# A hybrid decoder trunk on one core: the output projection's residual added by accumulating DMAs, with the banks copied out by ScalarE

## The chip, the cores and the metric

The kernel runs on one core of a Trainium2 chip. The metric is the time of one execution on the device in microseconds. The engines are TensorE (PE, with its weight loads as PEld), VectorE (DVE), ScalarE (ACT), GpSimd (POOL) and SyncE (SP). DMAs are issued here from SP's queue and from POOL's queue, and all run on the core's 16 DMA engines.

## The reference

Two layers of a trunk with 512 tokens and 2048 channels, all in float32. Each layer normalises x, projects it once, runs three groups of heads beside each other, and projects their gated outputs back onto x:

```python
for l in range(DEPTH):
    h = rmsnorm(x, norm_w[l])
    proj = jnp.einsum("bsd,de->bse", h, w_in[l])
    (ssd_z, ssd_xbc, ssd_dt, cfm_a, cfm_g, cfm_z,
     att_q, att_k, att_v, att_z) = jnp.split(proj, split_idx, axis=-1)
    y_ssd = ssd_branch(ssd_z, ssd_xbc, ssd_dt, ...)
    y_cfm = conformer_branch(cfm_a, cfm_g, cfm_z, ...)
    y_att = diff_attention_branch(att_q, att_k, att_v, att_z, ...)
    y = jnp.concatenate([y_ssd, y_cfm, y_att], axis=-1)
    x = x + jnp.einsum("bse,ed->bsd", y, w_out[l])
```

The change touches the last line: the sum of x and the output projection.

## The kernel before

Channels lie on the partitions. x is held as 16 blocks of 128 channels by 512 tokens, each in two parts whose sum is exact, `xh[k]` and `xl[k]` (`put_x`: ACT casts the block to `xh`, DVE subtracts to get `xl`, and the squares are summed for the norm).

All projections go through `project`. It fills four PSUM banks of 128 x 512 (`ps_p`, four buffers in all) from 16 blocks of the contraction, in eight steps of two blocks. For each step 512 KB of weights are loaded from SP's queue into `wraw` (two buffers), ACT scales and casts them to `wh` and DVE computes the remainder `wl` (four buffers each, so two steps), and PE runs 24 matmuls (lines 186 to 188): two blocks, four banks, three products of parts. In the last step the matmuls are sorted by bank, so that bank 0 is complete first and bank 3 last. The next chunk starts with a step in which each of the first 12 matmuls in turn reopens banks 0 to 3, three each, so a bank has to be emptied before its turn.

Work beside the projections is handed to `project` as a list of jobs, which are issued between the steps. The order of PE is that in which the code issues; on the other engines a scheduler of the framework orders instructions by priority and by its own estimate of when their inputs are there. `urgent()` raises the priority of weight splits and of the emptying of banks.

The output projection of a layer is four chunks (`dc`) of four blocks. Before the change, the job `res` has DVE add `xh[k]` and `xl[k]` into a tile `t` of the pool `rw` (four buffers) while the chunk is computed (line 774). When bank `b` is complete, DVE adds it to that tile (line 783). In layer 1 the tile is stored to `out` from SP (line 785). In layer 0 it is the new block of x: in the next chunk `dt_mm` multiplies the chunk's four tiles with the 16 columns for dt of the next layer (line 263, eight rows on PE in the trace, after the first step), and then four jobs `put_x` split them. The last chunk's tiles go into the first projection of layer 1 in the same way.

The instructions that the change concerns, in the file's words:

```python
for b in range(4):
    k = 4 * dc + b
    with urgent():
        V.tensor_tensor(ts[b], ts[b], banks[b], ALU.add)
    if l == DEPTH - 1:
        nc.sync.dma_start(out=out[k], in_=ts[b])
    else:
        jobs.append(lambda k=k, t=ts[b]: put_x(k, t))
```

Of the kernel before, what the change touches and what calls it, by code (L numbers as in the profile page):

```python
# [8 lines left out]
F32 = mybir.dt.float32  # L9
F32R = mybir.dt.float32r  # L10
AF = mybir.ActivationFunctionType
ALU = mybir.AluOpType
AX = mybir.AxisListType

P = 128
S = 512
D = 2048
KB = D // P
DEPTH = 2
EPS = 1e-6  # L20
NEG = -1e30
LEAD = 2000
# steps between the stages of what runs beside the projections
PL0, PL1, CL, QL, AL0, AL1, H0, HP, HL = 1, 2, 2, 2, 3, 1, 1, 5, 2
WARM = 2
TCUT, NPAD = (0, 7, 12, 18, 22, 26, 29, 32), 2

# one column chunk of the input projection per row: name, first column
CH_BC, CH_X0, CH_X1, CH_A, CH_G, CH_CZ, CH_Q, CH_K, CH_V, CH_AZ, CH_Z0, CH_Z1 = range(12)
CHUNK_COL = (2048, 1024, 1536, 2576, 3088, 3600, 4112, 4624, 5136, 5648, 0, 512)  # L30

# columns of the packed per-partition parameters
PP_CW, PP_CB, PP_SN, PP_FW, PP_FB, PP_LW, PP_LB, PP_SL = 0, 48, 60, 68, 192, 196, 200, 204
PP_N = 205
# columns of the packed row parameters (one layer)
RP_DTB, RP_AL, RP_QW, RP_KW, RP_LAM = 0, 16, 32, 96, 160
RP_N = 416
# columns of the constants
C_ID, C_TRI, C_STR, C_AM, C_ONE, C_DTS, C_ROPE = 0, 128, 256, 384, 512, 640, 656
C_N = 656 + 4 * 64  # L40

# [2 lines left out]
def kernel(  # L44
# [57 lines left out]
    sqx = [None]  # L102

    def add_sq(k, src):
        """The squares of x, summed over the blocks."""
        if k == 0:
            sqx[0] = lt([P, S], "rb")
            A.activation(sqx[0], src, AF.Square)
        else:
            t = sa()  # L110
            A.activation(t, src, AF.Square)
            V.tensor_tensor(sqx[0], sqx[0], t, ALU.add)

    def put_x(k, src):
        """x in two exact parts."""
        split(xh[k], xl[k], src)
        add_sq(k, src)

    pace, pace_hi = [None], [None]

    def weights(src, scales, raw=None, between=None):
        """Two 128-row blocks of weights: scaled by the row, in two exact parts."""
        with urgent():
            if raw is None:
                raw = wraw.tile([P, 2, S], F32, tag="wraw", name="wraw")
                nc.sync.dma_start(out=raw, in_=src)
            res = []
            for j in range(2):
                if j and between:
                    between()  # L130
                h = wsp.tile([P, S], F32R, tag="wh", name="wh")
                lo = wsp.tile([P, S], F32R, tag="wl", name="wl")
                if scales[j] is None:
                    split(h, lo, raw[:, j, :])
                else:
                    pace_hi[0] = A.activation(h, raw[:, j, :], AF.Copy, scale=scales[j]).ins  # L136
                    pace[0] = V.scalar_tensor_tensor(lo, raw[:, j, :], scales[j], h.bitcast(F32), ALU.mult,  # L137
                                                     ALU.subtract).ins
                res.append((h, lo))
        return res  # L140
# [1 line left out]
    clock, queue = [0], []  # L142

    def after(n, fn):
        """Issue fn n steps of the projections later."""
        queue.append((clock[0] + n, fn))

    def paced(fn):
        """Not before this step's weights are split."""
        with tc.issue_after(pace[0]):  # L150
            fn()

# [13 lines left out]
                fn()  # L166

    def project(src, order, act, scales, cm, jobs=(), pre=None):
        """Four [128, 512] sums over the 16 blocks; cm: channels on the partitions, else tokens.
        Jobs, and what they left for later, are issued between the steps."""  # L170
        banks = [ps_p.tile([P, S], F32, tag="ps_p", name="ps_p") for _ in range(4)]
        N = KB // 2
        for n, kk in enumerate(order):
            wt = weights(src[kk], scales[2 * kk:2 * kk + 2], *(pre(kk) if pre else ()))
            tick()
            order_jb = [(j, b) for j in range(2) for b in range(4)]
            if n == N - 1:
                order_jb.sort(key=lambda jb: jb[1])
            for j, b in order_jb:
                k = 2 * kk + j  # L180
                first, last = n == 0 and j == 0, n == N - 1 and j == 1
                h, lo = wt[j]
                ah, al = act[k]
                c = blk(b)
                if cm:
                    T.matmul(banks[b], h[:, c], ah, start=first, stop=False)  # L186
                    T.matmul(banks[b], h[:, c], al, start=False, stop=False)  # L187
                    T.matmul(banks[b], lo[:, c], ah, start=False, stop=last)  # L188
                else:
                    T.matmul(banks[b], ah[:, c], h, start=first, stop=False)  # L190
                    T.matmul(banks[b], ah[:, c], lo, start=False, stop=False)  # L191
                    T.matmul(banks[b], al[:, c], h, start=False, stop=last)  # L192
            for job in jobs[len(jobs) * n // N:len(jobs) * (n + 1) // N]:
                job()
        return banks

    def rsqrt_bcast(acc, n, tag):
        """1/sqrt(mean + eps) of column sums of squares, on every partition."""
        ps = psm()
        T.matmul(ps, ones, acc, start=True, stop=True)  # L200
        r = lt([P, S], tag)
        A.activation(r, ps, AF.Sqrt, scale=1.0 / n, bias=epst)
        V.reciprocal(r, r)
        return r

    # ---- parameters
    nc.sync.dma_start(out=nwt, in_=nw)
    # the array's clock rises while it waits for the first blocks
    z = sa()
    with tc.high_priority(2 * LEAD):  # L210
        V.memset(z, 0.0)
# [12 lines left out]
    first, xraw = [], []  # L224

    def load_x(kk, w):
        """Two blocks of x; the first two take turns with their weights."""
        if kk == 4:
            load_params()
        for k, t in first:  # L230
# [15 lines left out]
        split(xh[0], xl[0], first[0][1])  # L246
        return raw, lambda t=first[1][1]: split(xh[1], xl[1], t)

    # ---- the 16 dt columns, four blocks of x at a time side by side in the columns of the array
    psd, wd = [None], [None]  # L250

    def dt_load(l):
# [14 lines left out]
    for l in range(DEPTH):  # L267
# [47 lines left out]
        lead[0] = True  # L315

        def evac(banks, pad=0, rstd=rstd):
            """The banks times 1/rms(x), for channels on the partitions."""
            res = []
            with urgent():  # L320
                for b in banks:
# [4 lines left out]
                    res.append(t)  # L326
            return res

        # ---- dt = softplus(raw + bias), log1p by the series of atanh; a = -exp(a_log) dt and its sums
        sm64 = lambda tag: lt([P, 4, 16], tag)  # L330
        dt, s1, s2, s3, a_t, acs, dec, cdec = (sm64(n) for n in ("dt", "s1", "s2", "s3", "a_t", "acs", "dec", "cdec"))
        acr = [None]
# [42 lines left out]
            acr[0] = dram.tile([16, S], F32, name="acr")  # L375
            G.dma_start(out=acr[0], in_=r)

        # ---- causal convolution of x, B, C: channels on the partitions
        def conv4(raw, ci, dst, col=col):
            w = lambda j: col(PP_CW + 4 * ci + j)  # L380
            V.tensor_scalar(dst, raw[:, 3:3 + S], w(3), None, ALU.mult)
# [46 lines left out]
            after(CL, state)  # L428

        def ssd_pair(i, l=l, xs=xs, st=st, xdt=xdt, cbm=cbm, cT=cT, acs=acs, acr=acr):  # L430
            """Heads 2 i and 2 i + 1: within the chunks, then from the states before them."""
            g, j = i // 4, i % 4
            ms = [big.tile([P, S], F32, tag=f"o{2 * (i % 2) + half}", name="m") for half in range(2)]
            e = wt2()
# [47 lines left out]
        raws = evac(banks, 3)  # L482
        g1 = [lambda i=i, raws=raws: conv_x(i, raws) for i in range(4, 8)] + ssd_jobs(1)

        # ---- conformer: a * sigmoid(g), convolution, layer norm, silu
        u, ca = [], []
        banks = in_proj(CH_A, True, g0[8:] + g1[0:4])
        with urgent():
# [51 lines left out]
                V.tensor_tensor(ca[i], ca[i], rl, ALU.mult)  # L540
                A.activation(ca[i], ca[i], AF.Silu, scale=col(PP_LW + i), bias=col(PP_LB + i))

        # ---- attention: q, k normed and rotated, then transposed
        tabs = [None, None]

        def qk_tab(n, row=row, tabs=tabs):
# [54 lines left out]
        xq = evac_t(banks)  # L601
        banks = in_proj(CH_K, False, mix([ahead(lambda t=t, xq=xq: qk_norm(0, t, xq[t])) for t in range(4)], tp[1]))
        xk = evac_t(banks)
        # ---- differential attention over the keys up to each block of queries
        v, o = [], [None] * 4
        parts = [None] * 4

        def head(h, qk=qk, parts=parts):
            """q and k of one head in two exact parts: for each half, q high and low on the two halves of the
            partitions, k high on both, k low on both."""  # L610
            for half in range(2):
                own, other = slice(half * 64, half * 64 + 64), slice(64 - half * 64, 128 - half * 64)
                q_, k_ = qk[0][own, h, :], qk[1][own, h, :]
# [72 lines left out]
                A.activation(vt, banks[t], AF.Copy, scale=rstd_t[:, t:t + 1])  # L686
                v.append(vt)

        # ---- gate of the SSD group
        sqy = [None]  # L690

        def silus(raws):
# [68 lines left out]

        cjobs = [lambda raws=raws: silus(raws)] + [lambda i=i: cfm_out(i) for i in range(4)]

        # ---- output projection and residual
        sls = lt([P, 1], "sls")
        V.tensor_scalar(sls, col(PP_SL), 1.0 - lam_init, None, ALU.mult)
        out_scales = [col(PP_SN + i) for i in range(8)] + [None] * 4 + [sls] * 4
        jobs = cjobs + ([lambda l=l: dt_load(l + 1)] if l < DEPTH - 1 else [])
        for dc in range(4):
            ts = []  # L770

            def res(k, ts=ts):
                t = rw()
                V.tensor_tensor(t, xh[k].bitcast(F32), xl[k].bitcast(F32), ALU.add)
                ts.append(t)

            jobs = jobs + [lambda k=4 * dc + b, res=res: res(k) for b in range(4)]
            banks = project([w_out[l, dc, kk] for kk in range(KB // 2)], (0, 1, 2, 3, 6, 7, 4, 5), yact, out_scales, True, jobs)
            jobs = [lambda dc=dc, ts=ts: dt_mm(dc, ts)] if l < DEPTH - 1 else []
            for b in range(4):  # L780
                k = 4 * dc + b
                with urgent():
                    V.tensor_tensor(ts[b], ts[b], banks[b], ALU.add)
                if l == DEPTH - 1:
                    nc.sync.dma_start(out=out[k], in_=ts[b])
                else:
                    jobs.append(lambda k=k, t=ts[b]: put_x(k, t))
        late = jobs


# [59 lines left out]
```

## Time and profile before

| what | value |
|---|---|
| time, median of 3 runs | 1552.81 us (1552.58 to 1553.71) |
| span of the profiled execution | 1550.5 us |
| median of the runs less that span (what lies around the span) | 2.3 us |
| PE busy | 1543.9 us (100%) |
| PE weight loads busy | 1265.2 us (82%) |
| DVE busy | 1093.0 us (70%) |
| ACT busy | 719.1 us (46%) |
| POOL busy | 42.7 us (3%) |
| DMA from SP's queue | 143.75 MB, 30.9% of 16 engines |
| DMA from POOL's queue | 11.87 MB, 2.8% of 16 engines |

The profile is that of one execution; the span runs from its first to its last instruction. No total of that execution is listed beside its span, so the median of the runs stands for it. Busy shares are means over the whole span. A PE that is busy all the time is not at its peak: matmuls are pipelined, so a row lasts 0.39 us while the next one starts 0.23 us after it. Where PE has no idle time, its starts tell when a tile is needed.

### The profile page before, as it was taken

The page shows a single profiled execution, that of the slowest core. Times are in us where ns is not written, and L with a number is a line of the kernel's source. Part 1 is how long each engine was busy: PE and PEld are TensorE (multiplying, and loading weights), DVE is VectorE, ACT ScalarE, POOL GpSimd, SP SyncE. Part 2 cuts the span into 40 slices and gives each one's busy share as a digit, 9 for nine tenths or more (in the row PEclk, how much of TensorE's full clock was granted, in tenths as well). Part 3 has the DMA queues.
Part 4 walks back from the last instruction along what each step waited for, and adds up shares of the span by engine and source line. Part 5 has one row for each costly group of instructions (what it writes and reads, how often), then busy time and mean ns, then how long its engine had stood idle before and what let it go on. Part 6 is the DMA issues. An engine that isn't in the chain of part 4 may idle for free.

```text
span 1550.5 us, 19452 instructions
## 1 busy us (share of the span) xinstructions
PE 1543.9 (100%) x7220; PEld 1265.2 (82%) x7220; DVE 1093.0 (70%) x2040; ACT 719.1 (46%) x1176; POOL 42.7 (3%) x80
## 2 busy tenths in 40 slices
PE   9999999999999999999999999999999999999998
PEld 6788888888888888888888888888888888888887
DVE  7665756989698889543447667579897988883332
ACT  7442525334576667333244335253435766662221
POOL 0010100000000000000000101010000000000000
PEclk9999999999999999999999999999999999999999
DMA  7243333333322232333333434332333222334442
GB/s 244 82 134 94 112 115 113 94 96 87 100 76 79 82 86 96 95 96 95 95 95 85 131 87 133 101 113 88 96 96 87 77 82 83 83 94 123 124 126 76
DMA packets 47262, 156.85 MB, mean 101 GB/s; under 512 B 6496, under 2 KB 7392, under 8 KB 47168
## 3 DMA queue, kind: packets, MB, share of 16 engines
q1 hardware_dynamic: 42656, 143.75, 30.9%
q0 software_dynamic: 4512, 11.87, 2.8%
q8 instruction: 56, 0.92, 0.3%
q14 instruction: 38, 0.31, 0.1%
HBM read 151.34 MB, written 4.26 MB: 100 GB/s over the span
## 4 chain that ended last, share of the span: by engine, by line
PE 99%; DVE 0%; DMA 0%; issue 0%; SPq 0%; ACT 0%; DVEq 0%
PE ps_p L186 23%; PE ps_p L188 22%; PE ps_p L187 22%; PE ps_p L192 8%; PE ps_p L190 8%; PE ps_p L191 8%; PE ps_s L456 2%; PE ps_s L664 1%; PE ps_s L461 1%; PE ps_s L421 1%; PE ps_s L635 1%; PE ps_s L634 1%; PE ps_s L656 1%; PE ps_s L591 0%; PE ps_s L410 0%; PE ps_s L263 0%
## 5 line engine op out<-in xcount | busy, mean ns | idle before, releaser
L136 ACT ACTIVATE wh<-wraw,nwt 128x512 fp32r<-128x512 f32 x384 | 275.6, 722 | 459.6 <-PE ps_p L187 265.4
L186 PE MATMUL ps_p<-xh,wh 128*128 128x512 f32 x1024 | 411.8, 402 | 0.8 <-DVE rw L325 0.4
L188 PE MATMUL ps_p<-xh,wl 128*128 128x512 f32 x1024 | 400.4, 391 | 0.4 <-DVE wl L137 0.4
L187 PE MATMUL ps_p<-xl,wh 128*128 128x512 f32 x1024 | 399.6, 390 | 0.0
L137 DVE SCALAR_TENSOR_TENSOR wl<-wraw,nwt,wh 128x512 fp32r<-128x512 f32 x384 | 285.6, 748 | 152.1 <-ACT wh L136 149.3
L186 PEld LDWEIGHTS ps_p<-xh,wh 128*128 128x128 f32 x1024 | 192.8, 188 | 48.7 <-ACT wh L136 7.9
L187 PEld LDWEIGHTS ps_p<-xl,wh 128*128 128x128 f32 x1024 | 192.9, 188 | 41.4 <-issue 3.8
L188 PEld LDWEIGHTS ps_p<-xh,wl 128*128 128x128 f32 x1024 | 192.4, 188 | 41.8 <-DVE wl L137 1.1
L190 PE MATMUL ps_p<-wh,xh 128*128 128x512 f32 x512 | 202.8, 396 | 0.0
L192 PE MATMUL ps_p<-wh,xl 128*128 128x512 f32 x512 | 199.9, 390 | 0.0
L191 PE MATMUL ps_p<-wl,xh 128*128 128x512 f32 x512 | 199.6, 390 | 0.0
L510 DVE SCALAR_TENSOR_TENSOR ca<-u,ppt,ca 128x512 f32<-128x512 f32 x240 | 179.3, 747 | 2.9
L192 PEld LDWEIGHTS ps_p<-wh,xl 128*128 128x128 f32 x512 | 96.1, 188 | 20.3
L190 PEld LDWEIGHTS ps_p<-wh,xh 128*128 128x128 f32 x512 | 96.3, 188 | 18.9
L191 PEld LDWEIGHTS ps_p<-wl,xh 128*128 128x128 f32 x512 | 96.3, 188 | 18.8
L186 PE MATMUL ps_p<-ysh,wh 128*128 128x512 f32 x256 | 100.9, 394 | 0.0
L187 PE MATMUL ps_p<-ysl,wh 128*128 128x512 f32 x256 | 99.9, 390 | 0.0
L188 PE MATMUL ps_p<-ysh,wl 128*128 128x512 f32 x256 | 99.8, 390 | 0.0
L136 ACT ACTIVATE wh<-wraw,ppt 128x512 fp32r<-128x512 f32 x64 | 46.0, 722 | 85.5 <-PE ps_p L187 79.0
L137 DVE SCALAR_TENSOR_TENSOR wl<-wraw,ppt,wh 128x512 fp32r<-128x512 f32 x64 | 47.4, 747 | 49.6 <-ACT wh L136 49.5
L100 DVE TENSOR_TENSOR wl<-wraw,wh 128x512 fp32r<-128x512 f32 x32 | 22.2, 693 | 63.4 <-ACT wh L99 63.4
L137 DVE SCALAR_TENSOR_TENSOR wl<-wraw,sls,wh 128x512 fp32r<-128x512 f32 x32 | 24.0, 751 | 51.8 <-ACT wh L136 51.8
(450 smaller groups left out, 2013.5 us busy)
## 6 DMA issues: line engine op xcount, KB each, us to landing
wraw<-w_in SPq DMA_DIRECT2D x191, 512.0 KB, 3.6
wraw<-w_out SPq DMA_DIRECT2D x64, 512.0 KB, 3.6
m<-acr POOLq DMA_DIRECT2D x32, 256.0 KB, 4.3
xraw<-xT SPq DMA_DIRECT2D x16, 256.0 KB, 5.2
out<-rw SPq DMA_DIRECT2D x16, 256.0 KB, 2.7
wT<-acr POOLq DMA_DIRECT2D x32, 96.0 KB, 3.8
wraw<-w_in SPq DMA_DIRECT2D x2, 256.0 KB, 3.9
cst<-consts SPq DMA_DIRECT2D x1, 456.0 KB, 6.9
```

The source lines that it names most:

```text
L100: V.tensor_tensor(lo, src, hi.bitcast(F32), ALU.subtract)
L136: pace_hi[0] = A.activation(h, raw[:, j, :], AF.Copy, scale=scales[j]).ins
L137: pace[0] = V.scalar_tensor_tensor(lo, raw[:, j, :], scales[j], h.bitcast(F32), ALU.mult, ALU.subtract).ins
L186: T.matmul(banks[b], h[:, c], ah, start=first, stop=False)
L187: T.matmul(banks[b], h[:, c], al, start=False, stop=False)
L188: T.matmul(banks[b], lo[:, c], ah, start=False, stop=last)
L190: T.matmul(banks[b], ah[:, c], h, start=first, stop=False)
L191: T.matmul(banks[b], ah[:, c], lo, start=False, stop=False)
L192: T.matmul(banks[b], al[:, c], h, start=False, stop=last)
L421: T.matmul(ps, st[g][:, 3, blk(c)], dsx, start=True, stop=True)
L456: T.matmul(yd[half * 64:half * 64 + 64, blk(c)], xdt[g][c][:, hh:hh + 64], ms[half][:, blk(c)], start=True, stop=True)
L510: V.scalar_tensor_tensor(ca[i], u[i][:, j:j + S], w(j), ca[i], ALU.mult, ALU.add)
```

## The change

In all chunks but the last of layer 1, ACT copies the bank into the tile. In layer 0 a DMA from POOL's queue then adds the block of the input x to the tile, reading `xT` from memory (`accum_op=ADD` into the tile); the tile is used as before, and SP also stores it to `out`. In layer 1 the DMA from POOL's queue adds the tile onto what layer 0 has stored in `out`. The last four blocks of layer 1 keep the two adds on DVE, with the sum of the parts of x in tiles of the pool `big` (`xs_last`).

```diff
-        for dc in range(4):
-            ts = []
...
-            def res(k, ts=ts):
-                t = rw()
-                V.tensor_tensor(t, xh[k].bitcast(F32), xl[k].bitcast(F32), ALU.add)
-                ts.append(t)
...
-            jobs = jobs + [lambda k=4 * dc + b, res=res: res(k) for b in range(4)]
+        xs_last = []
+
+        def res(k, xs_last=xs_last):
+            t = big.tile([P, S], F32, tag=f"o{k % 4}", name="xlast")
+            V.tensor_tensor(t, xh[k].bitcast(F32), xl[k].bitcast(F32), ALU.add)
+            xs_last.append(t)
+
+        for dc in range(4):
+            jobs = jobs + [(lambda b=b: res(12 + b)) if l == DEPTH - 1 and dc == 3 else (lambda: None) for b in range(4)]
+            ts = []
...
+            last = l == DEPTH - 1 and dc == 3
             for b in range(4):
                 k = 4 * dc + b
+                t = rw()
                 with urgent():
-                    V.tensor_tensor(ts[b], ts[b], banks[b], ALU.add)
-                if l == DEPTH - 1:
-                    nc.sync.dma_start(out=out[k], in_=ts[b])
-                else:
-                    jobs.append(lambda k=k, t=ts[b]: put_x(k, t))
+                    if last:
+                        V.tensor_tensor(t, xs_last[b], banks[b], ALU.add)
+                        nc.sync.dma_start(out=out[k], in_=t)
+                    else:
+                        A.copy(t, banks[b])
+                        if l < DEPTH - 1:
+                            G.dma_start(out=t, in_=xT[k], accum_op=ALU.add)
+                            nc.sync.dma_start(out=out[k], in_=t)
+                        else:
+                            G.dma_start(out=out[k], in_=t, accum_op=ALU.add)
+                ts.append(t)
+                if l < DEPTH - 1:
+                    jobs.append(lambda k=k, t=t: put_x(k, t))
```

How it changes the order on ACT, at the end of the first chunk of layer 0's output projection. Before (the first two rows are the weight split of the next chunk's first step; `xh_91` to `xh_94` are blocks 0 to 3 of x; in brackets are the semaphores that a row waits for, by engine or DMA queue):

```order
L136 ACTIVATE wh<-wraw,ppt 128x512 [waits DMAHW2_49,DVE_49,PE_49]
L136 ACTIVATE wh<-wraw,ppt 128x512 [waits DVE_49,PE_49]
L99 CAST xh_91<-rw 128x512 [waits DVE_49]
L108 ACTIVATE rb<-rw 128x512
L99 CAST xh_92<-rw 128x512 [waits DVE_49]
L111 ACTIVATE sa<-rw 128x512
L136 ACTIVATE wh<-wraw,ppt 128x512 [waits DMAHW3_49,PE_49,Activation_49]
```

The same place after; a DMASW semaphore is that of a DMA from POOL's queue:

```order
L136 ACTIVATE wh<-wraw,ppt 128x512 [waits DMAHW2_49,DVE_49,PE_49]
L136 ACTIVATE wh<-wraw,ppt 128x512 [waits DVE_49,PE_49]
L790 COPY rw<-ps_p 128x512 [waits PE_49] x3
L136 ACTIVATE wh<-wraw,ppt 128x512 [waits DMAHW3_49,DVE_49,PE_49]
L99 CAST xh_91<-rw 128x512 [waits DMASW7_49]
L790 COPY rw<-ps_p 128x512 [waits PE_49]
L136 ACTIVATE wh<-wraw,ppt 128x512 [waits DVE_49]
L108 ACTIVATE rb<-rw 128x512
L99 CAST xh_92<-rw 128x512 [waits DMASW0_49]
```

Three banks are copied, then half of a weight split, then the cast of block 0 with a wait for its accumulating DMA, and only then the copy of the fourth bank and the other half of the split.

On PE, the dt matmuls after the first step of the next chunk, before (the rows follow the step's last matmul):

```order
L188 MATMUL ps_p<-ysh_5127,wl 128x512
L263 MATMUL ps_s<-rw,wd 32x512 [waits PE_49]
L263 MATMUL ps_s<-rw,wd 32x512 x3
L186 MATMUL ps_p<-ysh_5170,wh 128x512 [waits Activation_49]
L187 MATMUL ps_p<-ysl_5171,wh 128x512
```

and after:

```order
L188 MATMUL ps_p<-ysh_5127,wl 128x512
L263 MATMUL ps_s<-rw,wd 32x512 [waits DMASW7_49,PE_49]
L263 MATMUL ps_s<-rw,wd 32x512 [waits DMASW0_49]
L263 MATMUL ps_s<-rw,wd 32x512 [waits DMASW1_49]
L263 MATMUL ps_s<-rw,wd 32x512 [waits DMASW2_49]
L186 MATMUL ps_p<-ysh_5170,wh 128x512
```

Nothing moved on PE; each dt matmul now waits for the DMA of its own block.

On SP's queue, where before there were weight loads alone in layer 0's output projection, the stores of the four blocks now stand among them (the loads are those of steps 1 to 5 of the second chunk):

```order
L126 DMA wraw_5676<-w_out 128x1024 [waits DMAHW0_49,DVE_49]
L126 DMA wraw_5715<-w_out 128x1024 [waits DMAHW1_49,DVE_49]
L126 DMA wraw_5753<-w_out 128x1024 [waits DMAHW2_49,DVE_49]
L793 DMA out<-rw_5656 128x512 [waits DMASW7_49]
L793 DMA out<-rw_5660 128x512 [waits DMASW0_49]
L793 DMA out<-rw_5664 128x512 [waits DMASW1_49]
L126 DMA wraw_5792<-w_out 128x1024 [waits DMAHW3_49,DVE_49]
L793 DMA out<-rw_5668 128x512 [waits DMASW2_49]
L126 DMA wraw_5831<-w_out 128x1024 [waits DMAHW4_49,DVE_49]
```

The load of the fourth step follows three stores, that of the fifth a fourth store.

## Rows read from the trace of the kernel before

**Rows 1.** The page, busy time, share of the span, and instructions of an engine.

```profile
span 1550.5 us, 19452 instructions
PE 1543.9 (100%) x7220; PEld 1265.2 (82%) x7220; DVE 1093.0 (70%) x2040; ACT 719.1 (46%) x1176; POOL 42.7 (3%) x80
```

**Rows 2.** Waits of PE: line, who was waited for: total us, times, longest.

```profile
PE ps_s L215 <- DVE sa L211: 1.5, 1, 1.5
...
PE ps_p L186 <- ACT wh L136: 0.4, 1, 0.4
```

**Rows 3.** Busy time by stretch, layer 0's output projection, its four chunk seams.

```profile
core 0: us, PE busy (x) PEld busy (x) DVE busy (x) ACT busy (x) POOL busy (x), PEclk, DMA share, GB/s
646.00:691.00 45.00, 45.00 (x202) 36.25 (x201) 21.08 (x32) 15.59 (x25) 0.00 (x0) 1.00 0.32 94
...
781.00:826.00 45.00, 45.00 (x200) 35.95 (x199) 23.59 (x40) 16.38 (x24) 2.14 (x4) 1.00 0.31 94
```

**Rows 4.** The chain that ended last: start us, us, what; the dt matmuls.

```profile
652.01 0.99 PE ps_s L263 x8
...
786.67 1.00 PE ps_s L263 x8
```

**Rows 5.** Timeline of PE at the first seam: start us, us, engine, line, operation.

```profile
642.00 0.39 PE L188 MATMUL ps_p<-ych,wl 128*128 128x512 f32 x1
...
646.14 0.39 PE L188 MATMUL ps_p<-ych,wl 128*128 128x512 f32 x1
646.37 0.40 PE L186 MATMUL ps_p<-ysh,wh 128*128 128x512 f32 x1
...
648.45 0.39 PE L186 MATMUL ps_p<-ysh,wh 128*128 128x512 f32 x1
...
651.94 1.07 PE L263 MATMUL ps_s<-rw,wd 128*32 128x512 f32 x8
652.94 0.50 PE L186 MATMUL ps_p<-ysh,wh 128*128 128x512 f32 x1
```

**Rows 6.** Groups by line, DVE: busy us, mean ns | idle before, releaser.

```profile
L783 DVE TENSOR_TENSOR rw<-rw,ps_p 128x512 f32<-128x512 f32 x32 | 22.0, 686 | 15.5 <-PE ps_p L188 14.7
...
L774 DVE TENSOR_TENSOR rw<-xh,xl 128x512 f32<-128x512 f32 x32 | 20.5, 687 | 0.6 <-DMA out<-rw 0.6
```

**Rows 7.** Line 423, ACT's copy of a bank: duration ns min/median/max, first and last start.

```profile
L423 ACT COPY st<-ps_s x4: 586/588/589, 144.8 to 995.0; 128x512 f32<-128x512 f32 x4
```

**Rows 8.** Timeline at the end of the kernel.

```profile
1542.40 0.69 DVE L783 TENSOR_TENSOR rw<-rw,ps_p 128x512 f32<-128x512 f32 x1 [5.73 <-PE ps_p L188]
...
1543.12 4.47 SPq L785 DMA_DIRECT2D out<-rw  x4
```

**Rows 9.** Timeline of DVE at the first seam: banks 0 and 2.

```profile
642.43 0.69 DVE L783 TENSOR_TENSOR rw<-rw,ps_p 128x512 f32<-128x512 f32 x1
...
645.19 0.69 DVE L783 TENSOR_TENSOR rw<-rw,ps_p 128x512 f32<-128x512 f32 x1
```

**Rows 10.** Timeline of ACT at the first seam.

```profile
643.15 0.62 ACT L99 CAST xh<-rw 128x512 fp32r<-128x512 f32 x1 [1.60 <-DVE rw L783]
643.68 0.63 ACT L108 ACTIVATE rb<-rw 128x512 f32<-128x512 f32 x1
```

**Rows 11.** Line 437, loads of 256 KB from POOL's queue; the page's table of issues.

```profile
m<-acr POOLq DMA_DIRECT2D x32, 256.0 KB, 4.3
...
DMA to landing us min/median/max: 3.3/4.3/6.9
```

**Rows 12.** DMA issues of 85 to 87 us and of 89 to 90 us.

```profile
m<-acr POOLq DMA_DIRECT2D x1, 256.0 KB, 3.8
...
m<-acr POOLq DMA_DIRECT2D x1, 256.0 KB, 6.4
```

**Rows 13.** DMA rate in 40 slices of 640 to 665 us.

```profile
GB/s 0 0 0 0 0 105 203 393 138 0 0 0 0 0 0 164 249 361 66 0 0 0 0 177 256 321 85 0 0 0 0 0 0 111 164 374 184 7 0 0
```

**Rows 14.** The page's table of issues: weight loads, KB each, us to landing.

```profile
wraw<-w_out SPq DMA_DIRECT2D x64, 512.0 KB, 3.6
```

## What the change will do: the prediction

> **What bounds the kernel now.** I read the page first: TensorE (PE) is busy for 1543.9 of 1550.5 us [rows 1]. Then who kept PE waiting: four waits, between 1.5 us and 0.4 us, all in the start-up [rows 2]. Then the stretches that the change touches: in each of the four 45 us slices of layer 0's output projection (the first and the last stand) PE is busy for 45.00 us, while VectorE (DVE) is busy for about 21 and ScalarE (ACT) for about 16 [rows 3]. So in that place nothing but PE's own list of instructions sets the time. The work that the change takes off DVE lies beside it; the only thing that can move the end is a wait that PE does not have today. PE works in order and has no idle time to give back, so every microsecond of such a wait is added to the end.
>
> The question is therefore where PE meets the new transfers. The order of PE is the same before and after, so the clock times of the trace before serve as deadlines. I take the first seam (from output chunk 0 to chunk 1); in the trace the other three repeat it every 44.9 us: the dt matmuls stand there four times, from 652.01 to 786.67 [rows 4]. Deadlines at this seam [rows 5]: the last matmul into bank 0 starts at 642.00 and the last of the chunk, into bank 3, at 646.14. The next chunk starts at 646.37 and rewrites bank 3 from 648.45 on, so bank 3 has to be copied out by then. At 651.94 come eight rows of dt matmuls, two for each of the four sums `ts[b]`; they take 1.00 us, so the pair that reads `ts[3]` comes some 0.7 us in, at about 652.64.
>
> **The change part by part.**
>
> *Removed from DVE.* 28 of the 32 adds of the two parts of x (0.69 us each) and 28 of the 32 adds of bank and residual (0.69 us each), some 38 us of DVE time [rows 6]. All of it lies in stretches in which DVE is half idle and PE does not wait [rows 3]: worth nothing. The four adds that stay in the last chunk have another buffer; three of their x adds move some chunks ahead, under other DVE work. I cost that at nothing too, since PE waits for DVE nowhere after the start; if that cover were gone it would be 3 x 0.69 = 2 us.
>
> *Added to ACT.* 28 copies of a bank. The nearest row is the copy of a bank in L423, 0.59 us [rows 7]. 16.5 us in all, 4 x 0.59 per seam, on an engine that is busy for a third of the stretch. Layer 1 has nothing between its copies but weight splits, whose tiles are free in time; the same arrangement (banks read out by ACT in L560) leaves no wait on PE today. So layer 1's three seams cost nothing.
>
> *The tail.* The last four blocks still go bank, DVE add, store on SP. The four stores are issued from 1543.12 on [rows 8], as they will be. The last of the twelve accumulates into `out` of layer 1 is issued a whole chunk before the end, some 44 us (the 44.9 of a seam's period less 1.0 for the dt rows), and no instruction reads them: nothing.
>
> *Layer 0: the new path.* Before, `ts[b]` is complete 0.7 us after its bank. Now it is copy, issue on GpSimd's queue (POOL), an accumulating DMA of 256 KB that reads x, and its landing. Two things wait for landings. First, the dt matmuls wait for all four. Second, and this is what the order on ACT adds: the cast `xh_91<-rw`, which waits for block 0's landing, stands ahead of the copy of bank 3. Behind that cast are queued the copy of bank 3, so the fourth accumulate, and the second half of the next weight split. So two landings stand in series. I call L0 the time from issue to landing of the first accumulate, L3 that of the fourth.
>
> Copy of bank 0: starts at 642.43, when DVE's add starts today [rows 9], ends at 643.02. Issue 0.05 later (a store today is issued 0.03 after its add ends, 1542.40 + 0.69 to 1543.12 [rows 8]): 643.07. Landing: 643.07 + L0. Cast seen by ACT 0.05 later; the next instruction starts 0.53 behind a cast (643.15 to 643.68 [rows 10]); the copy of bank 3 takes 0.59: bank 3 is free at 644.24 + L0. Issue 0.05, landing L3, and 0.05 for the waiting PE: `ts[3]` is usable at 644.34 + L0 + L3. Against 652.64 the delay of one seam is
>
> D = L0 + L3 - 8.3 us, and nothing if that is negative.
>
> (Bank 3 by itself would hold PE from L0 = 4.2 on; where both waits occur the second contains the first.) The four seams have the same order, the fourth with the input projection of layer 1 behind it: the sum is 4 D.
>
> *What L is.* The trace has no accumulating DMA. The nearest rows are the 32 plain loads of the same size from the same queue, 128 rows of 2 KB: shortest 3.3, median 4.3, longest 6.9 us [rows 11]. The one issued into a quiet queue took 3.8, the last of eight issued in a row 6.4 [rows 12]. Below: 3.3 for both (an accumulate is not cheaper than the shortest plain load, since it reads its destination as well), D negative, cost 0. Above: twice the plain median, 8.6 for both, as if reading both operands doubled everything: D = 8.9, cost 36. I take a value near the plain one: the first at 3.8 to 4.3, plus a second read of 256 KB at the 393 GB/s that the busiest slice here moves [rows 13], 0.65 us: L0 = 4.9 as a rounded estimate. The fourth shares the DMA engines with the three stores of `out` that have now become due (256 KB each, another 0.65): L3 = 5.6. D = 4.9 + 5.6 - 8.3 = 2.2, and 4 D = 9.
>
> The Trainium skill's page "DMA: Bandwidth & Descriptors" (Anatomy of one DMA) fits a GpSimd-issued DMA as 2.0 us plus its bytes at 436 GB/s, which is 2.6 us for 256 KB as an estimate from that page; by it D would be negative and the change free. The traces of the plain loads disagree (3.3 at best [rows 11]).
>
> *SP's queue.* In layer 0 sixteen stores of `out` now stand on SP ahead of weight loads, each waiting for a landing. The load of the chunk's fourth step is queued behind the store of block 2, that of the fifth behind the store of block 3. Block 2's bank is ready 2.76 us after block 0's [rows 9], so its store goes at about 645.9 + 4.9 = 650.8. That load takes 3.6 us [rows 14] and would be there at 654.4; its split can begin only when the chunk's second step has ended on PE, past 658 (646.37 plus two steps of 5.4 and the dt rows). Slack some 4 us: cost nothing. If that cover goes, it costs PE one for one.
>
> **The rivals.**
>
> *Not slower* (the other side). The accumulates land like the quicker plain loads. One point decides: L0 + L3 under 8.3, that is 4.15 each; up to 3 us in all (D under 0.78, mean L under 4.5) it can't be told from no change. For it: plain loads of 3.6 to 4.3 exist [rows 11, 12], and so does a queue with gaps of 1.38 us between these accumulates. Against: the second read, and the plain median of 4.3 alone already gives D = 0.3. Time 1552.8, at most 1555.9. The page's fit named above gives this result.
>
> *Dear accumulates.* Reading the destination costs as much again as the transfer with its overhead: L = 8.6 each, D = 8.9, + 36, 1589. For it: nothing here shows how an accumulate goes, and the same queue shows 6.4 and 6.9 where it is loaded [rows 11, 12]. Against: most of a plain landing is no transfer time.
>
> *SP's queue takes over.* From landings of some 9 to 12 us on, the weight loads behind the stores come late as well. The seam sum alone is then 4 x (2 x 11 - 8.3) = 55: 1608 or more. For it only the unknown price.
>
> *That PE does not wait at all for the DMA* can be left out: the dt matmuls are listed with waits on the four landings.
>
> **How the numbers follow.** The profiled execution has a span of 1550.5 us, and the median of the runs is 1552.81, 2.3 more; I take these 2.3 us, which lie around the span, as unchanged. The span becomes 1559.5 and the time 1562 us. Chances: landings of 4.5 to 7 us, 1556 to 1575: 0.52. Not slower, 1552 to 1555.9: 0.22, and 0.03 for a gain over 0.2%, for which I see no mechanism. Dear accumulates, 1575 to 1597: 0.18. Beyond: 0.05. About 0.2% (3.1 us) is what a measurement of this kernel can tell from no change. That gives faster 0.03, same 0.22, slower 0.75, and a range from 1552 to 1590, which leaves out the gain, the far end of the dear case and what lies beyond it.
>
> **What would show it.** The waits of PE should list the dt matmuls (L263) waiting for DMA `rw<-xT` four times, about 1 to 2 us each, and the rewriting of bank 3 waiting for the ACT copy for under 1 us. ACT should wait for that DMA ahead of the cast of xh in each seam. The table of DMA issues should show `rw<-xT` at 4.5 to 6 us; that number decides all. Busy DVE time should fall by 38 us and bring nothing. I would be wrong if `rw<-xT` lands in 4 us or less (no change), in 8 or more (far slower), or if PE also shows waits in layer 1's output projection or on weights in layer 0.

## Result and profile after

Side by side on one chip the changed kernel takes 1564.44 us (median, 1563.36 to 1565.24), the kernel before 1552.94 us (1552.58 to 1553.71): a ratio of 1.0072 [1.006, 1.0084], so 11.5 us slower. The prediction was 1562. The profiled execution of after took 1565.24 us, with a span of 1563.5. That is 13.0 us over the span before, in the longest of the runs of after.

The page of after: first the busy time, share of the span and instructions of each engine (to be held against [rows 1]), then the DMA issues, out<-in, engine, count, KB each, median us from issue to landing:

```profile
span 1563.5 us, 19517 instructions
PE 1549.5 (99%) x7220; PEld 1264.6 (81%) x7220; DVE 1059.1 (68%) x1984; ACT 733.1 (47%) x1204; POOL 66.9 (4%) x108
...
out<-rw SPq DMA_DIRECT2D x20, 256.0 KB, 3.9
...
rw<-xT POOLq DMA_DIRECT2D x16, 256.0 KB, 5.4
out<-rw POOLq DMA_DIRECT2D x12, 256.0 KB, 6.1
```

VectorE (DVE) lost 34 us of work, and the kernel became slower. PE has the same 7220 instructions and 13.0 us more span. The accumulating DMA `rw<-xT` lands 5.4 us after its issue.

The waits of PE in after (line, who was waited for: us in total, times, longest), the answer to [rows 2]:

```profile
PE ps_s L263 <- DMA rw<-xT: 4.1, 4, 1.4
PE ps_p L186 <- ACT rw L790: 2.9, 4, 0.9
PE ps_s L215 <- DVE sa L211: 1.5, 1, 1.5
...
```

The first two lines are new, four times each: once per seam of layer 0's output projection. Nothing is new elsewhere. Busy time by stretch, the answer to [rows 3], says the same: 43.45 and 42.83 us of PE where 45.00 stood, at a granted clock of 1.00.

```profile
core 0: us, PE busy (x) PEld busy (x) DVE busy (x) ACT busy (x) POOL busy (x), PEclk, DMA share, GB/s
646.00:691.00 45.00, 43.45 (x190) 33.89 (x189) 16.09 (x23) 16.24 (x27) 1.76 (x3) 1.00 0.48 128
691.00:736.00 45.00, 42.83 (x187) 33.41 (x186) 15.68 (x23) 16.37 (x27) 3.42 (x4) 1.00 0.53 139
```

The two new waits add up to 7.0 us, and the span grew by 13.0. To see the rest I laid the start of each matmul of after beside that of the same matmul before. At the start of the first seam after is 0.49 us behind, nearly all of it from the start-up; the four seams add 2.90, 3.51, 2.44 and 3.51 us, 12.36 in all; layer 1 and the tail add 0.01. Here is the first seam on PE in after (start us, us, instruction, [idle before <-releaser]), beside [rows 5]:

```profile
648.72 0.39 PE L188 MATMUL ps_p<-ysh,wl 128*128 128x512 f32 x1
649.76 0.50 PE L186 MATMUL ps_p<-ysh,wh 128*128 128x512 f32 x1 [0.65 <-ACT rw L790]
650.09 0.39 PE L187 MATMUL ps_p<-ysl,wh 128*128 128x512 f32 x1
...
653.39 1.06 PE L263 MATMUL ps_s<-rw,wd 128*32 128x512 f32 x6
655.35 1.05 PE L263 MATMUL ps_s<-rw,wd 128*32 128x512 f32 x2 [0.90 <-DMA rw<-xT]
656.32 0.50 PE L186 MATMUL ps_p<-ysh,wh 128*128 128x512 f32 x1
```

Read the starts and not the idle times. From the start of the first dt matmul to the next L186 it is 653.39 to 656.32, 2.93 us, where before it was 651.94 to 652.94, 1.00: 1.93 lost, of which the wait line shows 0.90. The reason is that the dt matmuls of the four blocks run beside each other on PE. Of the eight rows, two for each block, the first of every block has begun by 652.00 in the kernel before, as its timeline of 651.9 to 652.0 shows:

```profile
651.94 0.64 PE L263 MATMUL ps_s<-rw,wd 128*32 128x512 f32 x4
```

All eight rows last 1.07 us there; after, the six rows of three blocks last 1.06 and the two of the fourth 1.05. So PE needs `ts[3]` at 651.94, together with the other three, and not 0.7 us later as the prediction took it; and the wait listed begins only when the rows of the other three blocks have ended. At bank 3 the starts stand 1.04 us apart (648.72 to 649.76), where the matmuls before them stand 0.22 to 0.24 apart, and the following start is 0.33 later: some 0.9 lost for 0.65 shown. Here each matmul lasts longer than the distance between starts, and the idle time is counted from the end of the row before.

The same seam on ACT and on GpSimd's queue (POOL) shows the chain. ACT first, beside [rows 10]:

```profile
642.92 0.59 ACT L790 COPY rw<-ps_p 128x512 f32<-128x512 f32 x1 [0.88 <-PE ps_p L188]
...
648.60 0.62 ACT L99 CAST xh<-rw 128x512 fp32r<-128x512 f32 x1 [1.71 <-DMA rw<-xT]
649.12 0.58 ACT L790 COPY rw<-ps_p 128x512 f32<-128x512 f32 x1
```

POOL, same view:

```profile
643.82 0.92 POOL L792 DMA_DIRECT2D rw<-xT  x1 [89.25 <-ACT rw L790]
645.19 0.87 POOL L792 DMA_DIRECT2D rw<-xT  x1 [0.45 <-ACT rw L790]
646.56 0.86 POOL L792 DMA_DIRECT2D rw<-xT  x1 [0.50 <-ACT rw L790]
650.00 0.85 POOL L792 DMA_DIRECT2D rw<-xT  x1 [2.58 <-ACT rw L790]
```

Copy of bank 0 until 643.51, issue at 643.82, landing 4.8 later, and the cast begins at 648.60; the copy of bank 3 stands behind the cast and ends at 649.70; PE gets bank 3 at 649.76; the fourth accumulate goes out at 650.00, lands 5.3 later, and PE gets `ts[3]` at 655.35. Two landings in series, as forecast.

### The profile page after: what moved, and what is told of

Read it like the earlier page. It is cut to its first block, busy times and chain, and to the rows that moved or that the text cites. A ratio compares the mean times of both kernels' runs of the same rounds, so it can differ in the third digit from the quotient of the medians.

```text
span 1563.5 us, 19517 instructions
## 1 busy us (share of the span) xinstructions
PE 1549.5 (99%) x7220; PEld 1264.6 (81%) x7220; DVE 1059.1 (68%) x1984; ACT 733.1 (47%) x1204; POOL 66.9 (4%) x108
## 4 chain that ended last, share of the span: by engine, by line
PE 82%; issue 13%; DMA 3%; DVE 1%; ACT 0%; SPq 0%; POOL 0%; POOLq 0%; DVEq 0%; ACTq 0%
PE ps_p L186 18%; PE ps_p L188 17%; PE ps_p L187 17%; PE ps_p L192 7%; PE ps_p L190 7%; PE ps_p L191 7%; DMA rw<-xT 2%; PE ps_s L456 1%; PE ps_s L664 1%; PE ps_s L461 1%; PE ps_s L421 1%; PE ps_s L635 1%; PE ps_s L634 1%; PE ps_s L656 1%; DMA out<-rw 1%
## 5 line engine op out<-in xcount | busy, mean ns | idle before, releaser
L186 PE MATMUL ps_p<-xh,wh 128*128 128x512 f32 x1024 | 411.5, 402 | 1.8 <-ACT rw L790 0.8
L186 PEld LDWEIGHTS ps_p<-xh,wh 128*128 128x128 f32 x1024 | 192.7, 188 | 50.3 <-ACT wh L136 7.5
L186 PE MATMUL ps_p<-ysh,wh 128*128 128x512 f32 x256 | 101.2, 395 | 2.1 <-ACT rw L790 2.1
```

## Experiments

The theory: nothing of the work that was moved costs time by itself; the cost is that PE meets two landings in series at each seam of layer 0, one through the cast that stands ahead of the copy of bank 3 on ACT, one directly at the dt matmuls. Rivals: the copies on ACT, the twelve accumulates into `out` of layer 1, or the stores on SP cost something; or the loads are as quick as plain ones and the order alone is to blame. Line numbers differ a little between kernels, since edits add lines.

**Layer 0 alone, and layer 1 alone.** Each half takes the new path in one layer, and the path of before (DVE's adds, and the store of the block) in the other. In e2_layer0:

```diff
+            new = l < DEPTH - 1
...
+                if new:
+                    t = rw()
+                    with urgent():
+                        A.copy(t, banks[b])
...
+                else:
+                    t = ts[b]
+                    with urgent():
+                        V.tensor_tensor(t, t, banks[b], ALU.add)
```

and in e3_layer1, where layer 0's blocks are also stored to `out` for layer 1 to add to:

```diff
+            new = l == DEPTH - 1 and dc < 3
```

> Layer 0 as in the changed kernel (copies by ACT, accumulating loads of x, stores of out), layer 1 as before the change (DVE adds, stores on SP). Theory of the landings (two landings in series ahead of the dt matmuls at each of layer 0's four seams): all of the cost is here, 1563 to 1566, that is 10 to 13 us over before, with the same eight waits of PE. Rival of the ACT copies (28 bank copies on ACT delay weight splits, 16 here and 12 in layer 1): about 16/28 of the loss, 1559.5. Rival of the accumulates into out (layer 1's DMAs cost): 1553 to 1558.

> Layer 1 as in the changed kernel (ACT copies, accumulates into out for three chunks, DVE for the last four blocks), layer 0 as before with a store of each block to out behind the DVE add. Theory of the landings: nothing on PE waits for a landing, 1552 to 1554. Rival of the ACT copies: 12/28 of the loss, 1558. Rival of SP's queue (stores in layer 0 ahead of weight loads cost by themselves): 1555 or more.

Layer 0 alone: 1563.80 us (1563.13 to 1564.53), 1.0070 [1.0053, 1.0087]. Layer 1 alone: 1552.67 (1552.39 to 1553.16), 0.9998 [0.9988, 1.0007]. Waits of PE in e2_layer0:

```profile
PE ps_s L263 <- DMA rw<-xT: 2.4, 4, 0.9
PE ps_p L186 <- ACT rw L786: 2.1, 4, 0.7
```

and the DMA issues in e3_layer1:

```profile
out<-rw SPq DMA_DIRECT2D x20, 256.0 KB, 2.8
...
out<-rw POOLq DMA_DIRECT2D x12, 256.0 KB, 5.7
```

All of the cost belongs to layer 0. Layer 1's twelve accumulates take 5.7 us each, and nobody waits for them; its copies on ACT and sixteen further stores on SP are free too.

**Plain loads in place of accumulates.** e4_plain leaves out layer 0's output projection from the x that layer 1 reads: the sixteen loads overwrite the tile. The order on all engines stays.

```diff
-                            G.dma_start(out=t, in_=xT[k], accum_op=ALU.add)
+                            G.dma_start(out=t, in_=xT[k])
```

> The changed kernel with the accumulate flag of the sixteen loads of x in layer 0 taken away, so the tile is overwritten by x (the output projection of layer 0 is left out of x): same queue, same place, same size, same stores, without the read of the destination. Theory of the landings: the plain load lands about 0.7 to 1 us earlier (4.3 to 4.6 in place of 5.4), and as two landings are in series each seam gets 1.5 to 2 us shorter: 1556 to 1559. Rival of the ACT copies or of the stores: 1564 as before. If the accumulate costs no more than a plain load: 1564.

1555.77 us (1554.49 to 1556.84), 1.0018 [1.0008, 1.0027]. What waits for line L792 and how long its DMAs take to land, in e4_plain (duration on the queue's engine min/median/max in ns, count):

```profile
L792 POOL DMA_DIRECT2D rw<-xT x16: 537/537/562, 643.5 to 784.1; - x16
...
PE ps_s L263: 0.4, 1
...
DMA to landing us min/median/max: 2.9/3.6/5.0
```

and the same view of after:

```profile
L792 POOL DMA_DIRECT2D rw<-xT x16: 848/859/919, 643.8 to 793.7; - x16
...
PE ps_s L263: 4.1, 4
...
DMA to landing us min/median/max: 4.7/5.4/5.9
```

The wait for bank 3 is gone altogether, and one wait at the dt matmuls is left; the four seams lose 0.39, 0.29, 0.18 and 1.47 us, 2.3 in all (in the first three the fourth block's rows start that much late beside the others, and no wait is listed). So the same order with transfers of the same size costs little: some 10 of the 12.4 us in the seams, or 8.7 of 11.5 between the medians, are the price of accumulating. The plain loads land sooner than expected (3.6 us, not 4.3 to 4.6), and the time is just below the range expected. In the first seam the first load lands in 3.7 us instead of 4.8.

**Without layer 0's stores to `out`.** e8_nostore is e2_layer0 less its sixteen stores on SP:

```diff
-                        nc.sync.dma_start(out=out[k], in_=t)
```

> As e2_layer0, without the sixteen stores of layer 0's blocks to out (not needed there, since layer 1 stores whole blocks). Theory of the landings: the waits stay; the fourth landing of a seam, which shares the DMA engines with three stores, gets up to 0.6 us shorter, so 1561 to 1564. Rival of the traffic (the stores and the queue behind them are the cost): 1553 to 1555.

1561.30 us (1559.76 to 1562.62), 1.0052 [1.0037, 1.0067]: some 2.5 us less than with them. Waits of PE in e8_nostore:

```profile
PE ps_p L186 <- ACT rw L786: 3.0, 4, 0.9
...
PE ps_s L263 <- DMA rw<-xT: 0.9, 1, 0.9
```

Bank 3 is still late, since the first landing is no shorter (4.7 to 5.0 in the four seams). The fourth takes 4.2, 4.1, 4.2 and 5.3 us, where it takes 5.1, 5.3, 4.7 and 5.0 in e2_layer0, which differs by the stores alone, and 5.3, 5.7, 4.9 and 5.8 in after. So the three stores that become due with it lengthen it by 0.6 us in the mean against e2_layer0, and by 1.0 against after; in the last seam e2_layer0 shows no such effect. One profile of each kernel does not settle it more closely.

**The cast behind the copy of bank 3.** e1_cast_later keeps everything, but the split of x of a chunk is ordered after the copy of that chunk's fourth bank:

```diff
+    def put_x_after(ins, k, src):
+        with tc.issue_after(ins):
+            put_x(k, src)
...
-                        A.copy(t, banks[b])
+                        copied[0] = A.copy(t, banks[b]).ins
...
-                    jobs.append(lambda k=k, t=t: put_x(k, t))
+                    jobs.append(lambda k=k, t=t, copied=copied: put_x_after(copied[0], k, t))
```

> The changed kernel with the casts of a chunk's blocks put behind the copy of its fourth bank on ACT, so that the first landing no longer stands ahead of the fourth. Theory of the landings: bank 3 is copied in time (no wait of PE on the copy), the fourth landing alone is left: copy done at about 647.8 by the clock of the trace before, issue 0.3 later, landing 5.4, against 652.64: 0.5 to 1.2 us a seam, 1555 to 1558. Rival of the ACT copies or of the traffic: 1564, as nothing is taken away.

1559.35 us (1559.08 to 1560.61), 1.0041 [1.0026, 1.0056]: it takes back 5.1 us, less than expected. Waits of PE, then two rows of the first seam on POOL (start us, us) in e1_cast_later:

```profile
PE ps_s L267 <- DMA rw<-xT: 1.8, 3, 1.1
```

```profile
644.20 0.92 POOL L797 DMA_DIRECT2D rw<-xT  x1 [89.25 <-ACT rw L795]
...
648.71 0.85 POOL L797 DMA_DIRECT2D rw<-xT  x1 [0.91 <-ACT rw L795]
```

Bank 3 holds PE no more, and the fourth accumulate goes out 4.5 us after the first instead of 6.2. The landings are not shorter (5.4, 5.5, 5.3, 6.2 for the fourth), and the seams still lose 1.35, 1.40, 1.19 and 2.15, 6.1 in all. The expectation missed by its deadline and not by the transfer: the fourth accumulate goes out no later than expected (648.71, in a trace that is 0.87 us behind at this seam, so 647.84 by the clock of the trace before; 648.1 expected). But PE needs the block at 651.94 and not at 652.64, as shown under the result; 0.7 us more in each seam gives 1.2 to 1.9.

**The dt matmuls one step later.** e6_dt_later puts an empty entry ahead of the dt matmuls in the list of jobs:

```diff
-            jobs = [lambda dc=dc, ts=ts: dt_mm(dc, ts)] if l < DEPTH - 1 else []
+            jobs = [lambda: None, lambda dc=dc, ts=ts: dt_mm(dc, ts)] if l < DEPTH - 1 else []
```

> The changed kernel with the dt matmuls one step (5.4 us) later in PE's list; the order on ACT stays. Theory of the landings: the dt matmuls no longer wait; the wait for bank 3, behind the first landing, stays at 0.7 to 1.1 us a seam: 1556 to 1558. If the dt matmuls are not where the time is lost: 1564.

1560.43 us (1559.39 to 1562.01), 1.0044 [1.0027, 1.0061], 2.4 us over the range expected. Waits of PE in e6_dt_later:

```profile
PE ps_p L186 <- ACT rw L790: 3.3, 4, 1.0
PE ps_p L186 <- DVE rw L325: 1.8, 2, 1.4
```

The wait at the dt matmuls is gone, and the seams lose 1.28, 1.08, 1.15 and 1.09, 4.6 in all, which is bank 3's wait alone. The second line was not foreseen: the empty entry shifts all jobs behind it by one step, the last splits of x among them, so layer 1's norm is late and PE waits for it at the end of layer 1's first projection (1.66 us). The profile is that of the longest run, 9.7 us over the span before; what the seams and the norm don't explain lies in the start-up (1.8 us), in layer 1 (0.4) and in the landing of the last store (1.2).

**Both edits.** e7_both has the two edits above together.

> Both edits together: casts behind the fourth copy, dt matmuls a step later; every copy, accumulate and store of the changed kernel stays. Theory of the landings: no wait of PE is left at the seams, 1552 to 1554, the time before the change. Rivals (ACT copies, traffic, or any cost of the work itself): above 1556.

1554.55 us (1554.31 to 1556.45), 1.0012 [1.0003, 1.0021]. Every seam loses 0.00. The late norm is left; first the waits of PE in e7_both, then the row on DVE that is late, then the same row in the kernel before (start us, us):

```profile
PE ps_p L190 <- DVE rw L329: 1.8, 2, 1.4
```

```profile
824.06 3.35 DVE L289 RECIPROCAL rstd<-rstd 128x512 f32<-128x512 f32 x1 [1.25 <-ACT rstd L288]
```

```profile
817.66 3.35 DVE L285 RECIPROCAL rstd<-rstd 128x512 f32<-128x512 f32 x1 [1.25 <-ACT rstd L284]
```

The reciprocal starts 6.4 us later; this trace is 0.95 behind from its start-up, so some 5.4, one step, come from the empty entry.

**Both edits, and the norm on time.** e9_both_norm_on_time is e7_both with the last two splits of x in one job, so that the jobs behind them stand where they stood:

```diff
+                    fn = lambda k=k, t=t, copied=copied: put_x_after(copied[0], k, t)
+                    if b == 3 and dc == 3:
+                        jobs[-1] = lambda a=jobs[-1], fn=fn: (a(), fn())
+                    else:
+                        jobs.append(fn)
```

> As e7_both, but in layer 1's first projection the last two blocks are split in one job, so that the sum for the norm (x_stats) stands again at the step where it stood before the change. In the trace of e7_both the four seams cost nothing and PE waits once, 1.4 us, for banks that wait for 1/rms(x) at the end of that projection, one step late. Theory: that wait goes, 1552.5 to 1553.5, no difference from before. Rival: the 1.4 us over before in e7_both come from the start-up or from the copies and accumulates themselves, 1554 to 1555.

1552.97 us (1552.50 to 1553.73), 0.9999 [0.999, 1.0008]. All waits of PE in e9_both_norm_on_time, its accumulating loads, the stretches in which after had lost time, and the busy time of its engines:

```profile
PE ps_s L219 <- DVE sa L215: 1.5, 1, 1.5
PE ps_p L190 <- ACT wh L140: 0.7, 1, 0.7
PE ps_p L190 <- DVE rw L329: 0.4, 1, 0.4
```

```profile
rw<-xT POOLq DMA_DIRECT2D x16, 256.0 KB, 5.7
```

```profile
646.00:691.00 45.00, 45.00 (x202) 36.23 (x201) 16.01 (x23) 17.67 (x30) 3.42 (x4) 1.00 0.51 140
691.00:736.00 45.00, 45.00 (x203) 36.19 (x202) 16.52 (x24) 17.55 (x29) 3.44 (x4) 1.00 0.52 141
```

```profile
PE 1544.3 (100%) x7220; PEld 1265.2 (82%) x7220; DVE 1058.8 (68%) x1984; ACT 733.6 (47%) x1204; POOL 67.0 (4%) x108
```

Every copy, accumulate and store of the change is in this kernel, its accumulates land no earlier than in after, and it is as fast as the kernel before: PE is busy for 45.00 of 45.00 us again. So the cost of the change was the place at which PE met the landings, and nothing else that these runs can tell (the interval is 0.1% to either side). It is no faster than before either: DVE's 34 us were hidden work.

**What stays open.** In several profiles the last seam, into layer 1's first projection, has a longer fourth landing than the others, with or without accumulation (5.0 against 3.5 to 3.9 in e4_plain, 6.2 against 5.3 to 5.5 in e1_cast_later), though not in e2_layer0 or e6_dt_later. Other transfers at the start of layer 1 may be the cause; that was not tried. Nor does a run show why accumulating takes 1.1 us more than a plain load.

## Why the prediction was right, step by step

- **PE bounds, and DVE's work is worth nothing.** Shown: DVE's busy time fell by 34 us (38 forecast: the 56 rows taken away last that long in sum, but some of DVE's rows overlap, and busy time counts them once) and the time rose; e9_both_norm_on_time has this saving without any new wait, and gains nothing.
- **Copies on ACT, layer 1, the tail: nothing.** Shown by e3_layer1 (0.9998) and by the 0.01 us that after loses behind the last seam. The copies are 0.59 us, as [rows 7] had it.
- **Two landings in series, the cast ahead of the copy of bank 3.** Shown: the rows of the seam above, step by step; e1_cast_later removes the first wait, e6_dt_later the second, both together remove the loss.
- **D = L0 + L3 - 8.3.** The form was right, the constant was off by 1.1. In after D = L0 + L3 - 7.2 gives every seam (4.8 + 5.3, 5.0 + 5.7, 4.7 + 4.9 and 4.9 + 5.8 give 2.9, 3.5, 2.4 and 3.5), and it gives the twelve seams of e2_layer0, e4_plain and e8_nostore within 0.05 us. Two parts of the constant were wrong. An issue from POOL starts 0.31 us after the copy ends (643.51 to 643.82, and 0.30 for the fourth), where I took the 0.05 of a store on SP: twice, 0.5 us. And the deadline for `ts[3]` was misread: the 1.00 us of the dt matmuls was shared out among four pairs in a row, which put the last pair at 652.64. They run beside each other from 651.94 on, and the last pair takes 0.97 us up to the next L186 (655.35 to 656.32), not 0.30: 0.7 us.
- **L0 = 4.9, L3 = 5.6.** Measured means 4.85 and 5.4. The sum came out almost right, in part by luck, since two errors cancel: the plain landing in this place is shorter than I took it (3.7 for the first in e4_plain, and I had started from 3.8 to 4.3), the accumulation dearer (1.1 us where I took 0.65 for the second read). The stores add 0.6 to 1.0 us to the fourth (0.65 taken).
- **The sum.** 4 x 2.2 = 9 forecast; 4 x 3.09 = 12.4 in the profile of after, and 11.5 between the medians. The error is the constant, 4 x 1.1, less what the landings were shorter. The range held although the constant was wrong: it was wide.
- **SP's queue: nothing.** Shown: no wait of PE on a weight in these stretches in after. The stores cost time only by way of the landing beside them (e8_nostore).
- **The rivals.** "Not slower" needed L0 + L3 below 8.3, in truth below 7.2; even plain loads stand a little above that (7.4 to 7.5 in three seams of e4_plain, 8.7 in the fourth), and their time, 1555.77, is within what that rival allowed. What excludes it is the price of accumulating. "Dear accumulates" (8.6 each) and "SP's queue takes over" are excluded by 4.7 to 5.9. The Trainium skill's fit ("DMA: Bandwidth & Descriptors", Anatomy of one DMA), 2.6 us for 256 KB as an estimate, is below every landing of 256 KB from POOL's queue measured here, plain ones (2.9 at best in e4_plain, 3.3 in the kernel before) included.

## What to carry to other kernels

Where the bounding engine has no idle time, work taken off another engine brings nothing, and each new transfer is to be judged by one question: at which instruction does the bounding engine meet its landing, and is the distance longer than the landing? Look for a wait that stands in an in-order queue ahead of something unrelated: here a cast that waited for a DMA held up the copy that frees a bank, and it was worth 5.1 of the 11.5 us to put it behind. To size a wait on TensorE, compare the starts of the same matmuls in both traces; the idle time listed showed 7.0 of 12.4 us here. And before you take a deadline from a merged row, look whether its instructions run one after the other or beside each other: the timeline of a short window tells how many have started.

## What the runs showed of the hardware

- A 256 KB load that adds to its destination lands 5.4 us after its issue (median, 4.7 to 5.9), the plain one in the same places 3.6 (2.9 to 5.0). The first of the first seam takes 4.8 against 3.7.
- It occupies POOL for 0.86 us instead of 0.54.
- An accumulate onto memory that holds `out` lands in 5.5 us (median, e9_both_norm_on_time) to 6.1 (after), a plain store from SP in 2.8 (e3_layer1).
- From the end of an ACT copy to the start of the issue on POOL it is 0.31 us; from the end of a DVE add to a store on SP it was 0.03 [rows 8].
- Three stores of 256 KB beside an accumulating load add 0.6 us (e8_nostore against e2_layer0) to 1.0 (against after) to its landing in the mean.
- The dt matmuls of four blocks, 32 columns of PE each, run beside each other: eight rows last 1.07 us, the six of three blocks 1.06, the two of one block 1.05.
